# A state-space layer's rotation and scan, moved into the PSUM banks that hold their input

## The chip, the cores and the metric

The kernel runs on one core of a Trainium2 chip. The metric is device time in microseconds (us) of one execution of the whole program, which is a two-block network of which the state-space layer is the first stage. Five engines matter: TensorE (PE, matmuls, and PEld, its weight loads), VectorE (DVE), ScalarE (ACT), GpSimd (POOL) and SyncE (SP), which issues the DMAs.

## What is computed

The reference is two transformer-like blocks. Only the first mixer, the state-space layer, is touched:

```python
def s5_mixer(u, lam_re, lam_im, log_dt, b_re, b_im, c_re, c_im, d_skip, w_glu):
    lam = lax.complex(lam_re.astype(f32), lam_im.astype(f32))
    dt = jnp.exp(log_dt.astype(f32))[:, None]
    a_bar = jnp.exp(lam * dt)
    b_bar = ((a_bar - 1.0) / lam)[..., None] * lax.complex(b_re.astype(f32), b_im.astype(f32))
    ug = u.astype(f32).reshape(bsz, length, S5_GROUPS, S5_GROUP).astype(jnp.complex64)
    bu = jnp.einsum('blgh,gph->blgp', ug, b_bar)
    a_seq = jnp.broadcast_to(a_bar, bu.shape)
    _, states = lax.associative_scan(_ssm_combine, (a_seq, bu), axis=1)
    c = lax.complex(c_re.astype(f32), c_im.astype(f32))
    y = jnp.einsum('blgp,ghp->blgh', states, c).real.reshape(bsz, length, D_MODEL)
    y = y + d_skip.astype(f32) * u.astype(f32)
    y = jax.nn.gelu(y).astype(u.dtype)
    val, gate = jnp.split(y @ w_glu, 2, axis=-1)
    return val * jax.nn.sigmoid(gate)
```

Length 512, model width 1024, 64 groups of 16 channels with 64 complex states each, all in fp32. Behind this layer follow its gated projection (`w_glu`), a feed-forward layer, sparse attention, a second feed-forward layer and the second block.

## The kernel before

`s5` (line 1172 on) works in chunks of 8 tokens. The 512 tokens are 64 chunks, so the scan over time is a scan over 64 chunk states. The 64 groups are cut into four rounds q = 0 to 3 of 16 groups (two halves t of 8 groups on the two halves of the partitions). In each round:

- `input_tables(q)` (three DVE products at L1384 into `raw`, `wH`, `wL`, then two POOL sums, L1390 and L1391) makes the complex input matrix `B`.
- `chunk(q)` (PE) transposes `B` (`btps`, copied out by ACT at L1443) and multiplies it with the input `U`: the two banks `vps` hold the real and imaginary contribution of each chunk, as `s.V`.
- `rotation(q)` (five POOL operations, L1426 to L1430) makes `cos` and `sin`.
- `states(q)` (14 DVE operations, L1492 to L1505) rotates `s.V` by `cos` and `sin`, so that the scan has a real factor, scans the two parts (L1499), and rotates back; ACT then copies the results `vr`, `vi` into `W` (L1510).
- `output_tables(q)` makes three more products on DVE (L1384, into `wL`, `Qi`, `Qr`) and `sums` two on POOL.
- `outputs(q)` (PE, tiles `yps`) multiplies `W` with `Q` and `U` with `toep` in two banks of 512 columns, ACT applies the gelu (L1527).
- `by_feature(q)` transposes the result (`yt`), and ACT and DVE split it into `xH` and `xL` (L178, L179).
- `kernel_of(q)` (PE, tile `kps`, 16 small matmuls with 32 columns each) makes the short convolution, which ACT copies (L1481) and a DMA writes as `toep`.

The rounds are pipelined by the loop at the end of `s5`: pass q issues, in this order, `input_tables(q+1)`, the sums of Q(q), `rotation(q+1)`, `outputs(q-1)`, `chunk(q+1)`, `states(q)`, `output_tables(q+1)`, `by_feature(q-1)`, `kernel_of(q+1)`. `in_order` fixes that order on DVE, POOL, ACT and PE, so each engine takes its own part of it strictly in turn. On PE one pass is therefore `yps` of round q-1, `btps` and `vps` of q+1, `yt` of q-1, `kps` of q+1. The gated projection (tiles `lin`, L33 to L35) begins on PE behind `outputs(3)`.

PSUM has eight banks: tag `pj` has four (here `vps` and `yps`, later `lin`), `sc` two (here `kps` and, ahead of the loop, `xps`), `tp` two. Scratch tiles of `states` (`mid_tmp`) come from a pool of six.

Of the kernel before, what the change touches and what calls it, by code (L numbers as in the profile page):

```python
# [75 lines left out]
def ps(k, name, tag="tp"):  # L76
    return k.psum.tile([P, 512], F32, tag=tag, name=name, bufs={"pj": 4, "sc": 2, "tp": 2}[tag])


def tmp(k, name="t", dt=F32):  # L80
    return k.tmp.tile([P, 512], dt, tag="tmp", name=name)
# [1090 lines left out]
def s5(k, x, next_gain):  # L1172
    nc, a = k.nc, k.a
    G2 = 32
    with ExitStack() as es:
# [17 lines left out]
        for n in ("s5_b_re", "s5_b_im"):  # L1193
            t_ = ep.tile([G2, 2, 64, 16], F32, name=n)
            v = a[n][0].rearrange("(q t i) p h -> t q i (p h)", q=4, t=2)
# [90 lines left out]
        for f in range(2):  # L1286
            for m in (1, 2, 4):
                n = m if f == 0 else min(m, 7 - m)
# [81 lines left out]
        for g in range(8):  # L1370
            b = ps(k, "ups", "pj")
# [29 lines left out]
        def mid_tmp(name):  # L1401
            return tmp(k, name).rearrange("p (a b) -> p a b", a=8)

        def big(name, bufs):
            return qp.tile([P, 1024], F32, tag=name, name=name, bufs=bufs)
# [80 lines left out]
        def flat(t):  # L1486
            return t.rearrange("p a b -> p (a b)")

        def states(q):
            s = st_[q]  # L1490
            vr, vi, w1, w2 = [mid_tmp(n) for n in ("vr", "vi", "w1", "w2")]
            nc.vector.tensor_mul(vi, s.V[1], s.cos)  # L1492
            nc.vector.tensor_mul(w2, s.V[0], s.sin)
            nc.vector.tensor_mul(vr, s.V[0], s.cos)
            nc.vector.tensor_mul(w1, s.V[1], s.sin)
            nc.vector.tensor_sub(vi, vi, w2)
            nc.vector.tensor_add(vr, vr, w1)
            for v in (vi, vr):
                nc.vector.tensor_tensor_scan(flat(v), flat(s.dec), flat(v), 0.0, op0=ALU.mult, op1=ALU.add)  # L1499
            nc.vector.tensor_mul(w1, vi, s.sin)  # L1500
            nc.vector.tensor_mul(w2, vi, s.cos)
            nc.vector.tensor_mul(vi, vr, s.sin)
            nc.vector.tensor_mul(vr, vr, s.cos)
            nc.vector.tensor_add(vi, vi, w2)
            nc.vector.tensor_sub(vr, vr, w1)  # L1505

            for w, z, sign in zip(W[q % 2], (vr, vi), (1.0, -1.0)):
                for t in range(2):
                    rows = slice(t * 64, t * 64 + 64)
                    s.done = nc.scalar.activation(w[rows, :, t, 1:], z[rows, :, :63], AF.Copy, scale=sign)  # L1510

        def outputs(q):
            s = st_[q]

            s.y = big("y", 2).rearrange("p (j i h) -> p j i h", j=8, i=8)
            for hh in range(2):
                b = ps(k, "yps", "pj")
                for i4 in range(4):
                    i = hh * 4 + i4
                    o = b[:, i4 * P:(i4 + 1) * P]  # L1520
                    for ri in range(2):
                        nc.tensor.matmul(o, W[q % 2][ri][:, i].rearrange("p t c -> p (t c)"),
                                         s.Q[ri][:, i].rearrange("p t h -> p (t h)"), start=ri == 0, stop=False)
                    for t in range(2):
                        rhs = s.toep.rearrange("p j (t i h) -> p t i j h", t=2, h=16)[:, t, i]
                        nc.tensor.matmul(o[t * 64:(t + 1) * 64], U[2 * q + hh][:, i4, t], rhs, start=False, stop=True)
                nc.scalar.activation(s.y[:, :, hh * 4:hh * 4 + 4].rearrange("p j i h -> p i j h"),  # L1527
                                     b.rearrange("p (i j h) -> p i j h", i=4, j=8), AF.Gelu_apprx_tanh)
# [51 lines left out]
        for q in range(5):  # L1580
            if q < 3:
                input_tables(q + 1)
            if q < 4:
                st_[q].Q = sums(st_[q].Q, nc.gpsimd)
            if q < 3:
                rotation(q + 1, nc.gpsimd)
            if q:
                outputs(q - 1)
            if q < 3:
                constants_of(q + 1)  # L1590
                chunk(q + 1)
            if q < 4:
                states(q)
            if q < 3:
                decay(q + 1)
                output_tables(q + 1)
            if q:
                by_feature(q - 1)
            if q < 3:
                kernel_of(q + 1)  # L1600
# [3 lines left out]
    w = a["s5_w_glu"][0]  # L1604
# [118 lines left out]
```

## Time and profile before

| | us |
|---|---|
| median of three runs | 2055.54 |
| lowest and highest of them | 2047.66, 2055.92 |
| the profiled execution | 2055.45 |
| its span | 2053.7 |

The profile is of one execution. [...] The four rounds lie between 53 and 169 us of the span.

### The profile page before, as it was taken

The page shows a single profiled execution, that of the slowest core. Times are in us where ns is not written, and L with a number is a line of the kernel's source. Part 1 is how long each engine was busy: PE and PEld are TensorE (multiplying, and loading weights), DVE is VectorE, ACT ScalarE, POOL GpSimd, SP SyncE. Part 2 cuts the span into 40 slices and gives each one's busy share as a digit, 9 for nine tenths or more (in the row PEclk, how much of TensorE's full clock was granted, in tenths as well). Part 3 has the DMA queues.
Part 4 walks back from the last instruction along what each step waited for, and adds up shares of the span by engine and source line. Part 5 has one row for each costly group of instructions (what it writes and reads, how often), then busy time and mean ns, then how long its engine had stood idle before and what let it go on. Part 6 is the DMA issues. An engine that isn't in the chain of part 4 may idle for free. (4 is left out here: it accounts for less than half of the span.)

```text
span 2053.7 us, 25075 instructions
## 1 busy us (share of the span) xinstructions
PE 1905.5 (93%) x9383; PEld 1582.3 (77%) x9383; DVE 1166.4 (57%) x2082; ACT 818.7 (40%) x1461; POOL 454.6 (22%) x466
## 2 busy tenths in 40 slices
PE   4779999999998878999999999999999879999997
PEld 3657888888887867877888888877787658888886
DVE  8983444324357997787443334477776675333443
ACT  3333333213234437675322123355565364233232
POOL 6850111101114644533111011112221120000001
PEclk9668999999999989999999999999999889999999
DMA  3012333233323231222333232343232213332332
GB/s 77 24 45 93 94 93 101 93 102 93 97 83 83 57 89 43 57 61 77 102 93 102 93 103 87 98 131 92 77 93 72 80 34 93 97 98 93 103 93 82
DMA packets 183938, 173.44 MB, mean 84 GB/s; under 512 B 11953, under 2 KB 178297, under 8 KB 183816
## 3 DMA queue, kind: packets, MB, share of 16 engines
q1 hardware_dynamic: 183048, 170.98, 27.9%
q8 instruction: 74, 1.21, 0.2%
q0 software_dynamic: 768, 0.86, 0.2%
q14 instruction: 48, 0.39, 0.1%
HBM read 158.92 MB, written 2.13 MB: 78 GB/s over the span
## 5 line engine op out<-in xcount | busy, mean ns | idle before, releaser
L127 DVE TENSOR_TENSOR wL<-raw,wH 128x1024 fp32r<-128x1024 f32 (+4 forms) x282 | 327.8, 1163 | 470.3 <-ACT wH L126 470.0
L126 ACT ACTIVATE wH<-raw 128x1024 fp32r<-128x1024 f32 (+4 forms) x314 | 308.5, 984 | 586.7 <-PE lin L34 430.1
L33 PE MATMUL lin<-xH,wH 128*128 128x512 f32 x1312 | 518.1, 395 | 6.0 <-ACT wH L126 2.4
L35 PE MATMUL lin<-xH,wL 128*128 128x512 f32 x1312 | 514.3, 392 | 5.2 <-DVE wL L127 5.2
L34 PE MATMUL lin<-xL,wH 128*128 128x512 f32 x1312 | 514.6, 392 | 0.0
L33 PEld LDWEIGHTS lin<-xH,wH 128*128 128x128 f32 x1312 | 248.5, 189 | 57.7 <-ACT wH L126 4.6
L35 PEld LDWEIGHTS lin<-xH,wL 128*128 128x128 f32 x1312 | 247.6, 189 | 57.4 <-DVE wL L127 6.8
L34 PEld LDWEIGHTS lin<-xL,wH 128*128 128x128 f32 x1312 | 248.2, 189 | 49.9 <-issue 0.5
L35 PE MATMUL lin<-hH,wL 128*128 128x512 f32 x608 | 236.7, 389 | 0.0
L33 PE MATMUL lin<-hH,wH 128*128 128x512 f32 x608 | 236.6, 389 | 0.0
L34 PE MATMUL lin<-hL,wH 128*128 128x512 f32 x608 | 236.5, 389 | 0.0
L325 POOL TENSOR_TENSOR up<-up,ga 128x512 f32<-128x512 f32 x44 | 75.3, 1711 | 542.1 <-DVE up L324 542.1
L286 POOL TENSOR_TENSOR acc<-acc,sq 128x512 f32<-128x512 f32 x42 | 63.1, 1502 | 592.3 <-ACT sq L285 591.4
L34 PEld LDWEIGHTS lin<-hL,wH 128*128 128x128 f32 x608 | 114.1, 188 | 23.8
L33 PEld LDWEIGHTS lin<-hH,wH 128*128 128x128 f32 x608 | 114.1, 188 | 23.7
L35 PEld LDWEIGHTS lin<-hH,wL 128*128 128x128 f32 x608 | 114.1, 188 | 23.4
L33 PE MATMUL qkv<-wH,xH 128*128 128x384 f32 x256 | 91.7, 358 | 2.8 <-ACT sqv L662 2.8
L34 PE MATMUL qkv<-wL,xH 128*128 128x384 f32 x256 | 90.4, 353 | 1.3 <-POOL wL L127 1.3
L35 PE MATMUL qkv<-wH,xL 128*128 128x384 f32 x256 | 89.8, 351 | 0.0
L178 ACT ACTIVATE hH<-up 128x512 fp32r<-128x512 f32 x44 | 27.9, 633 | 147.5 <-POOL up L325 147.5
L179 DVE TENSOR_TENSOR hL<-up,hH 128x512 fp32r<-128x512 f32 x44 | 30.5, 692 | 88.0 <-ACT hH L178 88.0
L421 POOL TENSOR_SCALAR p<-p,r 128x128 f32<-128x128 f32 (+1 forms) x96 | 52.8, 567 | 121.8 <-DVE r L419 91.2
(456 smaller groups left out, 2941.9 us busy)
## 6 DMA issues: line engine op xcount, KB each, us to landing
raw<-in_ffn_w_gate_up SPq DMA_DIRECT2D x88, 512.0 KB
raw<-in_ffn_w_down SPq DMA_DIRECT2D x40, 512.0 KB
raw<-in_w_up SPq DMA_DIRECT2D x32, 512.0 KB
raw<-in_w_down SPq DMA_DIRECT2D x28, 512.0 KB
raw<-in_dsa_w_in SPq DMA_DIRECT2D x96, 128.0 KB
raw<-in_w_in SPq DMA_DIRECT2D x20, 512.0 KB
raw<-in_s_w_glu SPq DMA_DIRECT2D x16, 512.0 KB
k<-k SPq DMA_DIRECT2D x30, 256.0 KB
```

Of the source, the lines that this page charges most:

```text
L33: nc.tensor.matmul(out, wH, xH, start=start, stop=False)
L34: nc.tensor.matmul(out, wH, xL, start=False, stop=False)
L35: nc.tensor.matmul(out, wL, xH, start=False, stop=stop)
L126: nc.scalar.activation(wH, raw, AF.Copy)
L127: (l_engine or nc.vector).tensor_sub(wL, raw, wH.bitcast(F32))
L178: k.nc.scalar.activation(outH, src, AF.Copy)
L179: k.nc.vector.tensor_sub(outL, src, outH.bitcast(F32))
L286: (nc.vector if d == KT - 1 else nc.gpsimd).tensor_add(k.acc, k.acc, sq)
L325: nc.gpsimd.tensor_mul(u, u, acts[m])
L421: nc.gpsimd.tensor_scalar(p, p, r[:, b:b + 1], 1.0, op0=ALU.mult, op1=ALU.mult)
```

## The change

`states` no longer copies the rotated parts out to SBUF. It names the two PSUM banks of `s.V` A and B, writes two of the four products of the first rotation to scratch and the other two back into A and B, subtracts and adds into A and B, scans A and B in place, and rotates back with A and B as source and partly as target. There are 14 operations before and after. Each of them now has one input in PSUM and one in SBUF; eight write to PSUM. The scratch tile `w2` is gone. `outputs` takes its two banks from tag `sc` in place of `pj`.

```diff
         def states(q):
             s = st_[q]
-            vr, vi, w1, w2 = [mid_tmp(n) for n in ("vr", "vi", "w1", "w2")]
-            nc.vector.tensor_mul(vi, s.V[1], s.cos)
-            nc.vector.tensor_mul(w2, s.V[0], s.sin)
-            nc.vector.tensor_mul(vr, s.V[0], s.cos)
-            nc.vector.tensor_mul(w1, s.V[1], s.sin)
-            nc.vector.tensor_sub(vi, vi, w2)
-            nc.vector.tensor_add(vr, vr, w1)
-            for v in (vi, vr):
+            vr, vi, w = [mid_tmp(n) for n in ("vr", "vi", "w1")]
+
+            A, B = s.V
+            nc.vector.tensor_mul(vi, B, s.cos)
+            nc.vector.tensor_mul(vr, A, s.cos)
+            nc.vector.tensor_mul(A, A, s.sin)
+            nc.vector.tensor_mul(B, B, s.sin)
+            nc.vector.tensor_sub(A, vi, A)
+            nc.vector.tensor_add(B, vr, B)
+            for v in (A, B):
                 nc.vector.tensor_tensor_scan(flat(v), flat(s.dec), flat(v), 0.0, op0=ALU.mult, op1=ALU.add)
-            nc.vector.tensor_mul(w1, vi, s.sin)
-            nc.vector.tensor_mul(w2, vi, s.cos)
-            nc.vector.tensor_mul(vi, vr, s.sin)
-            nc.vector.tensor_mul(vr, vr, s.cos)
-            nc.vector.tensor_add(vi, vi, w2)
-            nc.vector.tensor_sub(vr, vr, w1)
+            nc.vector.tensor_mul(w, A, s.sin)
+            nc.vector.tensor_mul(A, A, s.cos)
+            nc.vector.tensor_mul(vi, B, s.sin)
+            nc.vector.tensor_mul(B, B, s.cos)
+            nc.vector.tensor_add(vi, vi, A)
+            nc.vector.tensor_sub(vr, B, w)
...
-                b = ps(k, "yps", "pj")
+                b = ps(k, "yps", "sc")
```

On DVE, round 0, the middle of `states` before (`vi`, `vr`, `w1`, `w2` are SBUF scratch, `vps` PSUM, `dec` the scan's factor in SBUF):

```order
L1495 TENSOR_TENSOR w1_761<-vps_551,sin_486 128x512
L1496 TENSOR_TENSOR vi_760<-vi_760,w2_762 128x512 [waits DVE_49]
L1497 TENSOR_TENSOR vr_759<-vr_759,w1_761 128x512 [waits DVE_49]
L1499 SCALAR_TENSOR_TENSOR vi_760<-dec_584,vi_760 128x512 [waits DVE_49,Activation_49]
L1499 SCALAR_TENSOR_TENSOR vr_759<-dec_584,vr_759 128x512 [waits DVE_49]
L1500 TENSOR_TENSOR w1_761<-vi_760,sin_486 128x512 [waits DVE_49]
```

and the same place now:

```order
L1497 TENSOR_TENSOR vps_551<-vps_551,sin_486 128x512
L1498 TENSOR_TENSOR vps_534<-vi_760,vps_534 128x512 [waits DVE_49]
L1499 TENSOR_TENSOR vps_551<-vr_759,vps_551 128x512 [waits DVE_49]
L1501 SCALAR_TENSOR_TENSOR vps_534<-dec_584,vps_534 128x512 [waits DVE_49,Activation_49]
L1501 SCALAR_TENSOR_TENSOR vps_551<-dec_584,vps_551 128x512 [waits DVE_49]
L1502 TENSOR_TENSOR w1_761<-vps_534,sin_486 128x512 [waits DVE_49]
```

The place in the program and the number of operations are the same; from the subtraction on, one of the two inputs of each is a PSUM bank where both were SBUF tiles. No instruction of POOL, ACT or SP moves.

On PE, the second half of `chunk(2)` before (`btps` are the transposes of `B`, `U4` and `U5` inputs):

```order
L1442 MATMUL btps_891<-ident_73,wH_820 128x128 [waits Activation_49]
L1442 MATMUL btps_891<-ident_73,wH_820 128x128 x3
L1442 MATMUL btps_897<-ident_73,wH_820 128x128 [waits Activation_49]
L1442 MATMUL btps_897<-ident_73,wH_820 128x128 x3
L1450 MATMUL vps_903<-U4_453,raw_877 64x64 x8
L1450 MATMUL vps_903<-U5_460,raw_877 64x64 x8
```

and now:

```order
L1442 MATMUL btps_890<-ident_73,wH_819 128x128 [waits Activation_49]
L1442 MATMUL btps_890<-ident_73,wH_819 128x128 x3
L1442 MATMUL btps_896<-ident_73,wH_819 128x128 [waits Activation_49]
L1442 MATMUL btps_896<-ident_73,wH_819 128x128 x3
L1450 MATMUL vps_902<-U4_453,raw_876 64x64 [waits DVE_49]
L1450 MATMUL vps_902<-U4_453,raw_876 64x64 x7
L1450 MATMUL vps_902<-U5_460,raw_876 64x64 x8
```

The order is the same; the first `vps` matmul of rounds 2 and 3 now waits until DVE has finished with the bank, which `states` of two rounds before holds to its end. The `yps` matmuls, in the other two banks, wait for ACT (the last reader of those) where they waited for DVE.

## Rows read from the trace of the kernel before

**Rows 1.** The page's first part: busy us, share, instructions.

```profile
PE 1905.5 (93%) x9383; PEld 1582.3 (77%) x9383; DVE 1166.4 (57%) x2082; ACT 818.7 (40%) x1461; POOL 454.6 (22%) x466
```

**Rows 2.** By windows: PE, PEld, DVE, ACT, POOL busy, PE clock, DMA.

```profile
76.80:91.80 15.00, 14.53 (x64) 9.81 (x64) 15.00 (x12) 4.14 (x7) 10.72 (x4) 0.50 0.13 39
...
105.20:116.10 10.90, 10.43 (x46) 7.15 (x46) 9.64 (x14) 4.24 (x10) 3.57 (x2) 0.50 0.19 55
116.10:118.40 2.30, 2.30 (x21) 1.59 (x20) 2.30 (x1) 0.00 (x0) 2.30 (x2) 1.00 0.03 4
...
173.50:250.00 76.50, 76.50 (x339) 63.31 (x338) 26.81 (x29) 25.41 (x31) 7.05 (x5) 1.00 0.32 103
```

**Rows 3.** Timeline of PE, 67 to 169 us: start, us, instruction, idle before.

```profile
67.72 0.39 PE L1479 MATMUL kps<-cbd,wH 128*128 128x32 f32 x2
76.78 0.77 PE L1522 MATMUL yps<-Qr,W 128*128 128x128 f32 x2 [8.67 <-issue]
...
91.82 1.97 PE L1442 MATMUL btps<-ident,wL 128*128 128x128 f32 x8
...
105.20 0.77 PE L1522 MATMUL yps<-Qr,W 128*128 128x128 f32 x2 [1.06 <-issue]
...
118.45 1.09 PE L1442 MATMUL btps<-ident,wL 128*128 128x128 f32 x8
...
136.56 0.77 PE L1522 MATMUL yps<-Qr,W 128*128 128x128 f32 x2 [7.07 <-issue]
...
154.13 0.63 PE L1522 MATMUL yps<-Qr,W 128*128 128x128 f32 x2
...
168.61 0.80 PE L33 MATMUL lin<-xH,wH 128*128 128x512 f32 x1
```

**Rows 4.** Waits, 45 to 170 us: us in total, times, longest.

```profile
ACT W L1510 <- DVE vr L1505: 32.6, 3, 13.0
```

**Rows 5.** Timeline of DVE, round 0 and the start of round 1.

```profile
53.55 0.68 DVE L1492 TENSOR_TENSOR vi<-vps,cos 128x512 f32<-128x512 f32 x1
...
55.94 2.78 DVE L1496 TENSOR_TENSOR vi<-vi,w 128x512 f32<-128x512 f32 x1
58.65 2.83 DVE L1497 TENSOR_TENSOR vr<-vr,w 128x512 f32<-128x512 f32 x1
61.41 3.38 DVE L1499 TENSOR_TENSOR_SCAN vi<-dec,vi 128x512 f32<-128x512 f32 x1
...
75.25 1.21 DVE L1384 TENSOR_TENSOR wL<-pw,cv 128x1024 f32<-128x1024 f32 x1
...
82.06 0.68 DVE L1492 TENSOR_TENSOR vi<-vps,cos 128x512 f32<-128x512 f32 x1
```

**Rows 6.** Timeline of POOL over the same stretch.

```profile
52.58 3.28 POOL L1390 TENSOR_TENSOR wH<-raw,wH 128x1024 f32<-128x1024 f32 x1 [3.60 <-DVE wH L1384]
55.82 2.36 POOL L1391 TENSOR_TENSOR wL<-raw,wL 128x1024 f32<-128x1024 f32 x1
58.13 2.81 POOL L1390 TENSOR_TENSOR Qi<-wL,Qi 128x1024 f32<-128x1024 f32 x1
...
63.67 2.37 POOL L1426 TENSOR_TENSOR r<-rt,rsum 128x512 f32<-128x512 f32 x1
...
71.87 1.70 POOL L1430 TENSOR_TENSOR sin<-r,sin 128x512 f32<-128x512 f32 x1
```

**Rows 7.** Timeline of DVE, round 3.

```profile
141.37 0.68 DVE L1492 TENSOR_TENSOR vi<-vps,cos 128x512 f32<-128x512 f32 x1
...
143.76 0.68 DVE L1496 TENSOR_TENSOR vi<-vi,w 128x512 f32<-128x512 f32 x1
...
144.96 1.21 DVE L1499 TENSOR_TENSOR_SCAN vi<-dec,vi 128x512 f32<-128x512 f32 x1
...
150.45 0.68 DVE L1505 TENSOR_TENSOR vr<-vr,w 128x512 f32<-128x512 f32 x1
```

**Rows 8.** Timeline of ACT, the first copies into W.

```profile
75.42 1.25 ACT L1510 ACTIVATE W<-vr 64x504 f32<-64x504 f32 x2 [13.01 <-DVE vr L1505]
```

**Rows 9.** Groups of DVE by line, 53 to 152 us: busy, mean ns | idle.

```profile
L179 DVE TENSOR_TENSOR xL<-yt,xH 128x256 fp32r<-128x256 f32 x8 | 3.2, 422 | 2.5 <-ACT xH L178 2.5
```

## The prediction

> **What bounds the kernel now.** Read the page first: PE is busy 93% of the span, DVE 57%, POOL 22% [rows 1]. So whatever shortens DVE work is worth nothing unless PE stands waiting for it. The view by windows then shows two regimes. From 173.5 us on PE is busy for the whole of each window at full clock (76.50 of 76.50 us); before that, in the four rounds of the state-space layer, it works at half clock for long stretches and has holes [rows 2]. Then read the timeline of PE for the holes. From the end of `kps` of round 1 at 67.72 + 0.39 = 68.11 us to the first `lin` matmul at 168.61 us there are three idle times worth the name: 8.67 us ahead of `outputs(0)`, 1.06 us ahead of `outputs(1)`, 7.07 us ahead of `outputs(2)`, 16.80 us in all [rows 3]. All three end when `W` is there: in this stretch ACT's copies into `W` waited three times for the last DVE operation of `states`, 32.6 us in total [rows 4]. The bound of the layer is thus the loop DVE `states` to ACT `W` to PE `outputs`, and what the change can take off the end is at first these 16.80 us. `lin` starts as soon as PE is through with `outputs(3)`, and behind it PE is full, so an earlier `lin` moves everything behind it.
>
> **Why states is slow.** The DVE timeline of round 0 has two kinds of rows. The four products that read a PSUM bank take 0.68 us, though POOL is working (its L1390 runs from 52.58 to 55.86 us). The subtraction and addition behind them, with both inputs in SBUF, take 2.78 and 2.83 us and the first scan 3.38 us [rows 5, 6]. Each stalled row ends about half a microsecond after a POOL instruction has ended: L1496 ends at 58.72, POOL's L1391 at 58.18 [rows 5, 6]. So the two engines take turns, one instruction each, at something that they share. In round 3, where POOL has nothing left to do, the very same rows take 0.68 and 1.21 us [rows 7]. The whole of `states` takes 150.45 + 0.68 - 141.37 = 9.8 us there, and 75.25 - 53.55 = 21.7 us in round 0, of which 12 us are stalls; rounds 1 and 2 look the same.
>
> **What the change removes.** After it every operation of `states` has one input in PSUM and one in SBUF. The row for that is the product from `vps`, which is not stalled [rows 5]. I take 9.8 us for each round, so `states` ends 12 us sooner in rounds 0 to 2. What the trace does not show is an operation that writes to PSUM, and a scan on it. The lower bound is the free row of the same shape, 0.68 us and 1.21 us for a scan; below that nothing goes, since the element count is unchanged. The upper bound is the stalled row, 2.8 and 3.4 us. I take the lower one, because reading PSUM at all costs nothing there: 0.68 us from PSUM against 0.68 us from SBUF [rows 5, 7].
>
> [...]
>
> **What comes late next: DVE and POOL.** The stalls don't vanish altogether, they move. `states(0)` now ends at 53.55 + 9.8 = 63.3 us. POOL's four sums run beside it without turns: 52.58 + 3.28 + 3 x 2.31 = 62.8 us (2.31 us is the unstalled row, 55.82 to 58.13) [rows 6]. Behind it DVE has six table products with both inputs in SBUF, 1.21 us each, and POOL the five rotation operations. These ran 63.67 to 73.57 us with turns taken; without the five DVE turns of 0.5 to 1 us in them I put them at 6.2 us. Taking turns, both need 6.2 + 6 x 1.21 = 13.5 us from 62.8, so `states(1)` starts near 76 us, where it was 82.06 [rows 5, 6]. At worst, rotation 9.9 us and then the tables 7.3 us, it is 80 us.
>
> **What comes late next: PE.** PE reaches `outputs(0)` at 68.1 us. It needs the first copies into `W`; ACT takes 1.25 us for the two [rows 8], so they are there at 63.3 + 1.3 = 64.6 us and PE no longer waits. The slack is 3.5 us. `outputs(0)` then takes its 15.04 us (76.78 to 91.82), to 83.2 us. `chunk(2)` behind it needs `B(2)`, two POOL sums (4.6 us) after 76, 80.6 us: no wait. `btps` to `kps` took 105.20 - 1.06 - 91.82 = 12.32 us, so PE is at 95.5 us when it comes to `outputs(1)`. `W(1)` is held back not by `states(1)` (76 + 9.8 = 85.8) but by ACT, which has the copies of `btps` ahead of it, to about 88 us; it is there by 89.3. So the second hole goes too. Next `outputs(1)`, 13.25 us (105.20 to 118.45), to 108.7 us. Meanwhile DVE has run round 1: tables and rotation as above, four `xL` pieces, (3.2 + 2.5) / 2 = 2.9 us [rows 9], and `input_tables(3)`, whose `wH` waits for `kps(2)` at 95.5; `states(2)` starts near 98 us. `W(2)` is ready by about 114 us, behind ACT's copies again; PE comes to `outputs(2)` at 108.7 + (136.56 - 7.07 - 118.45 = 11.04) = 119.7 us. The third hole goes. `outputs(2)`, `yt` and `outputs(3)` take 168.61 - 136.56 = 32.05 us, to 151.8 us [rows 3]. `states(3)`, which starts near 120 us behind `xL(1)`, ends near 130 us; ACT copies `W(3)` behind the gelu of `outputs(2)`, as before.
>
> The added waits are covered: `vps` of rounds 2 and 3 waits for the end of `states` two rounds before (63.3 against 83 us, 86 against 109), and `yps` in tag `sc` waits for `kps` or gelu copies that precede it on ACT by microseconds. If one of these failed, PE's whole queue would stand behind it; nothing in the times above comes closer than 3 us.
>
> **The sum.** 68.1 + 15.04 + 12.32 + 13.25 + 11.04 + 32.05 = 151.8 us for the first `lin`, in place of 168.6: 16.8 us less, exactly the three holes. Against the profiled execution, 2055.45 us, that is 2038.6 us; the median of the runs, 2055.54, is the same number. I say 2038.
>
> **The rivals.** (1) *PE's clock rises in `outputs`.* Its matmuls ran at 0.50 nearly throughout; only for the last 2.3 us of `outputs(1)`, 11 us after it had begun, was it 1.00 [rows 2]. `outputs(1)` was also the one that followed `kps` after only 1.06 us of idling, the two after 7 and 8.7 us stayed at half. With the holes gone all follow closely. At full clock one `outputs` takes about 8 us (two of its eight pieces took 2.0 us in those 2.3), 6.5 to 7 us less. One such stage gives 2031.5; if all four rise, DVE and POOL bound rounds 1 to 3 and `lin` starts near 138 us, 2025. The three times of before, one of them 8 us under the others, may be this. Against it: 32 us of closely packed `outputs(2)` and `outputs(3)` did not raise it.
>
> (2) *The turns take the place of the stalls.* If tables and rotation cost their upper bound each round, `states(1)` starts at 80, `states(2)` near 108, `states(3)` near 135 us and ends at 145; `W(3)` is there at 146, and `outputs(3)` begins at 146.5 in place of 154.1. Then 7.6 us are left of the gain: 2048. For it: all six tables have both inputs in SBUF. Against it: the turns in rows 5 and 6 cost DVE no more than the POOL instruction in front.
>
> (3) *It does not do what it says*: an operation with one SBUF input that writes to PSUM takes turns with POOL as before. Then nothing moves: 2055. The unstalled `vps` products speak against it.
>
> (4) *Slower.* The in-place banks have their own price: reading and writing one bank slows each PSUM-writing operation, in round 3 too, where nothing was stalled. Count six 512-column operations and two scans at two units each, ten units. The three uncontended rounds are then 3 x (9.8 + d) + 22 us of tables and `xL`, so `states(3)` ends at 53.55 + 51.4 + 3d + 9.8 + d = 115 + 4d. It ended at 151.1, so it decides from d = 9 us, 0.9 us a unit, on (0.6 now). At 1.2 us a unit, d = 12, `states(3)` ends at 163 us and the kernel takes about 2066. For it: no row shows such a write. Against: it must cost two and a half times a free operation.
>
> **How the numbers follow.** The forecast (2033 to 2044) gets 0.53, the rising clock (2024 to 2033) 0.23, the turns (2044 to 2051) 0.13, no effect (about 2055) 0.06, slower 0.05. About 0.5%, 10 us, is what a measurement of this kernel tells from no change. Faster by more than that (below 2045) is the forecast and the clock: 0.76; slower 0.05; the rest, 0.19, within. The range reaches down to 2026, leaving out the case that all four stages rise, and up to 2048, which takes in rival (2) and leaves (3) and (4) out.
>
> **What would show it.** The rows of `states` at 0.68 and 1.2 us in all four rounds (else rival 3 or 4); table products of up to 2.7 us beside POOL's rotation; the holes ahead of `outputs(0)`, `(1)` and `(2)` gone; the first `lin` at 152 us; the stretch behind it as long as before. The prediction is wrong if a hole stays, if the clock in `outputs` is not 0.50, or if the time from the first `lin` to the end changes by more than a few us.

## The result and the profile after

The changed kernel takes 2026.17 us (median of four runs, 2024.39 to 2026.96), beside 2053.97 us (2047.66 to 2055.92) for the kernel before: a ratio of 0.9874, 95% interval 0.9856 to 0.9891. That is 27.8 us less, where 16.8 us less were forecast: 2026.17 lies 0.17 us above the lower end of the range, in the band of rival (1) and not in the forecast of 2033 to 2044. The profiled execution took 2024.39 us with a span of 2022.6.

First the operations of `states`. The timeline of DVE, after, round 0, the scans of round 3 and the tables behind round 0 (start, us, instruction):

```profile
53.56 0.69 DVE L1494 TENSOR_TENSOR vi<-vps,cos 128x512 f32<-128x512 f32 x1
...
55.96 0.69 DVE L1498 TENSOR_TENSOR vps<-vi,vps 128x512 f32<-128x512 f32 x1
56.55 0.69 DVE L1499 TENSOR_TENSOR vps<-vr,vps 128x512 f32<-128x512 f32 x1
57.15 2.34 DVE L1501 TENSOR_TENSOR_SCAN vps<-dec,vps 128x512 f32<-128x512 f32 x2
...
62.97 2.36 DVE L1384 TENSOR_TENSOR wL<-pw,cv 128x1024 f32<-128x1024 f32 x1
65.25 2.48 DVE L1384 TENSOR_TENSOR Qi<-pw,cv 128x1024 f32<-128x1024 f32 x1
...
74.46 1.21 DVE L1384 TENSOR_TENSOR wL<-bw,bt 128x1024 f32<-128x1024 f32 x1
75.59 0.68 DVE L1494 TENSOR_TENSOR vi<-vps,cos 128x512 f32<-128x512 f32 x1
...
120.35 2.33 DVE L1501 TENSOR_TENSOR_SCAN vps<-dec,vps 128x512 f32<-128x512 f32 x2
```

The subtraction and addition take 0.69 us where they took 2.78 and 2.83, two scans together 2.34 us where the first alone took 3.38 [rows 5]. They are as fast in round 0, with POOL at work, as in round 3, where it is nearly done. `states(0)` takes 62.97 - 53.56 = 9.4 us in place of 21.7. The stalls have moved to the table products, 1.21 us before [rows 5], now 2.3 to 2.5 us five times out of six: those are the ones that lie beside POOL's rotation. `states(1)` starts at 75.59 us, before at 82.06.

POOL, after, the same stretch. Its sums, 2.81 us each when DVE took turns with them [rows 6], run at 2.35; rotation is what now takes turns:

```profile
58.16 2.35 POOL L1390 TENSOR_TENSOR Qi<-wL,Qi 128x1024 f32<-128x1024 f32 x1
...
62.78 1.46 POOL L1426 TENSOR_TENSOR r<-rt,rsum 128x512 f32<-128x512 f32 x1
64.21 2.44 POOL L1427 TENSOR_TENSOR sin<-rsum,rt 128x512 f32<-128x512 f32 x1
```

The timeline of PE, after, answers [rows 3]:

```profile
69.60 0.77 PE L1524 MATMUL yps<-Qr,W 128*128 128x128 f32 x2
...
80.26 1.09 PE L1442 MATMUL btps<-ident,wL 128*128 128x128 f32 x8 [0.22 <-POOL wL L1391]
...
90.85 0.47 PE L1524 MATMUL yps<-Qr,W 128*128 128x128 f32 x2
...
102.55 1.97 PE L1442 MATMUL btps<-ident,wL 128*128 128x128 f32 x8 [2.09 <-POOL wL L1391]
...
113.95 0.78 PE L1524 MATMUL yps<-Qr,W 128*128 128x128 f32 x2
...
127.64 0.46 PE L1524 MATMUL yps<-Qr,W 128*128 128x128 f32 x2 [1.45 <-issue]
...
141.14 0.50 PE L33 MATMUL lin<-xH,wH 128*128 128x512 f32 x1
```

No idle time stands ahead of `outputs(0)`, `(1)` and `(2)` any more; ahead of and inside `outputs(3)` PE still waits 1.45 and 0.77 us for `W(3)`. The first `lin` comes at 141.1 us, before at 168.6: 27.5 us, against 16.8 forecast. The other 3.6 us of the two profiles' spans (2053.7 and 2022.6) lie behind the first `lin`, 1885.1 us before and 1881.5 after. That is within the scatter of that stretch: a kernel of the old kind below (`x_sc`) has 2046.0 - 164.2 = 1881.8 us there, the changed kernel in a second profile 2023.9 - 139.2 = 1884.7, and all kept profiles lie between 1881.5 and 1885.1.

What the forecast did not have is in the view by windows, after, for the four `outputs` (PE, PEld, DVE, ACT, POOL busy, PE clock, DMA):

```profile
69.60:80.00 10.40, 10.40 (x65) 7.25 (x65) 10.40 (x11) 2.26 (x3) 9.24 (x4) 0.74 0.19 57
90.80:100.40 9.60, 9.60 (x66) 6.72 (x65) 8.70 (x13) 1.96 (x5) 7.02 (x5) 0.82 0.14 38
113.90:124.40 10.50, 10.50 (x66) 7.31 (x65) 9.60 (x17) 1.96 (x5) 7.53 (x4) 0.74 0.19 58
127.60:141.10 13.50, 12.69 (x64) 8.77 (x64) 3.78 (x6) 5.12 (x9) 0.00 (x0) 0.62 0.25 79
```

The stages took 15.0, 13.3, 15.1 and 14.5 us at a clock of 0.50 nearly throughout [rows 2, 3]. Now they take 10.4, 9.6, 10.4 and 13.5 us at mean clocks of 0.62 to 0.82, that is, part of each at a clock of 0.50 and part at 1.00, the full one in this view. `outputs(0)`, for one, had 0.50 from 69.6 to 73.2 us, and `outputs(1)` 1.00 from 90.8 to 92.0 and 0.50 from 92.0 to 94.0. The timelines show it by the pace of the first two matmuls of a piece, 0.80 us at 0.50 and 0.49 at 1.00; the very first two of a stage took 0.77 and 0.46 to 0.47.

### The profile page after: what moved, and what is told of

It reads as the page before. It is cut to its first block, busy times and chain, and to the rows that moved or that the text cites. A ratio compares the mean times of both kernels' runs of the same rounds, so it can differ in the third digit from the quotient of the medians.

```text
span 2022.6 us, 25073 instructions
## 1 busy us (share of the span) xinstructions
PE 1890.0 (93%) x9383; PEld 1571.9 (78%) x9383; DVE 1142.5 (56%) x2082; ACT 819.3 (41%) x1461; POOL 451.7 (22%) x466
## 3 DMA queue, kind: packets, MB, share of 16 engines
q8 instruction: 74, 1.21, 0.3%
```

## The experiments

My theory after the result had two parts. (a) A DVE operation with two SBUF inputs takes turns with POOL, instruction by instruction, and one with a PSUM input does not; the change takes `states` out of these turns, `W` comes earlier, and PE's holes close. (b) With the holes closed PE's clock rises within `outputs`, which gives the part that was not forecast. The rivals: the other banks for `yps` carry the gain; SBUF inputs are slow as such; the clock's rise has nothing to do with the holes.

### The banks: x_sc and x_pj

`x_sc` is the kernel before with the tag alone changed, `x_pj` the changed kernel with the tag alone taken back:

```diff
-                b = ps(k, "yps", "pj")
+                b = ps(k, "yps", "sc")
```

> The kernel before with one line changed: the yps banks come from tag sc. My theory (the gain comes from DVE operations that no longer take turns with POOL, and from what follows of it on PE) expects nothing here: states 21.7 us in rounds 0 to 2, the three PE holes of 8.7, 1.1 and 7.1 us, the first lin near 168.6 us, about 2054 us. The rival, that the other banks free the PE order, expects smaller holes and 5 us or more less.

> The changed kernel with the yps banks back in tag pj, so the four pj banks hold both vps and yps. vps of rounds 2 and 3 then has to wait for the end of states of the round just before (85.4 and 107.3 us in the changed kernel, where vps began at 83.6 and 106.0). Theory: 2 to 3 us more on PE, the states rows unchanged at 0.69 us, 2026 to 2030 us. Rival, that the move of yps carries the gain: 2045 us or more.

`x_sc` took 2053.3 us, ratio 0.9998 (0.9987 to 1.0010); `x_pj` 2027.73 us, 0.9873 (0.9854 to 0.9893). So the banks for `yps` carry nothing; the whole gain is in `states`. In `x_pj` the wait that I had expected for `vps` isn't there: `vps` of round 2 ran from 83.0 to 85.1 us without idling, and the first `lin` came at 140.6 us. Its `outputs` took 12.6, 13.7, 13.5 and 9.2 us, though PE had not idled ahead of any of them. `outputs(1)` even began at the pace of the full clock, 0.47 us, and then fell to 0.80; the same pair of matmuls in the first and in the second piece of the stage:

```profile
90.24 0.47 PE L1524 MATMUL yps<-Qr,W 128*128 128x128 f32 x2
...
91.41 0.80 PE L1524 MATMUL yps<-Qr,W 128*128 128x128 f32 x2
```

The profile of `x_sc` brought something else. Its `states` started at 53.55, 82.05, 113.42 and 141.35 us, as before, but its `outputs` took 12.0, 15.1, 11.2 and 11.8 us, the first `lin` came at 164.2 us, and that execution was the quickest of its ten, 2047.74 us. The holes ahead of the four stages were 9.73, 4.29, 5.30 and 2.90 us. Behind the longest of them `outputs(0)` began at the slow pace, 0.77 us, and went over to 0.49 half way:

```profile
76.77 0.77 PE L1522 MATMUL yps<-Qr,W 128*128 128x128 f32 x2 [9.73 <-issue]
...
84.69 0.49 PE L1522 MATMUL yps<-Qr,W 128*128 128x128 f32 x2
```

The length of `outputs` thus varies from execution to execution of one and the same kind of kernel, which fits the 8 us between the runs of the kernel before. It also varies with and without holes, so theory (b) can't be the whole of it.

### Which operations take turns: x_scan and x_rotb

In `x_scan` two of the 14 operations get two SBUF inputs again:

```diff
-            nc.vector.tensor_sub(A, vi, A)
-            nc.vector.tensor_add(B, vr, B)
-            for v in (A, B):
-                nc.vector.tensor_tensor_scan(flat(v), flat(s.dec), flat(v), ...
+            nc.vector.tensor_sub(vi, vi, A)
+            nc.vector.tensor_add(vr, vr, B)
+            for v, z in ((A, vi), (B, vr)):
+                nc.vector.tensor_tensor_scan(flat(v), flat(s.dec), flat(z), ...
```

> The changed kernel, but the subtraction and addition ahead of the scans write to SBUF scratch and the scans read both inputs there (output in the PSUM banks). Exactly two of the 14 operations of states then have two SBUF inputs. Theory (turns are taken per instruction, by its two SBUF inputs): these two rows 2.4 to 3.4 us in rounds 0 to 2 and 1.2 in round 3, the other twelve 0.69; states 13 us; PE has the slack, so the first lin moves by 0 to 3 us, 2025 to 2030 us. Rival (PSUM output, or all SBUF traffic, decides): the scans stay at 1.2 us, states 9.8 us.

The timeline of DVE in `x_scan`, round 0:

```profile
56.52 0.68 DVE L1499 TENSOR_TENSOR vr<-vr,vps 128x512 f32<-128x512 f32 x1
57.12 2.15 DVE L1501 TENSOR_TENSOR_SCAN vps<-dec,vi 128x512 f32<-128x512 f32 x1
59.18 3.31 DVE L1501 TENSOR_TENSOR_SCAN vps<-dec,vr 128x512 f32<-128x512 f32 x1
62.41 0.67 DVE L1502 TENSOR_TENSOR w<-vps,sin 128x512 f32<-128x512 f32 x1
```

Exactly the two scans are stalled, with their output in PSUM as in the changed kernel; their neighbours are not. Rounds 1 and 2 show the same (2.1 and 3.3 us). It is the inputs that decide. On the time I was wrong: 2035.4 us (2028.12 to 2038.3), ratio 0.9904 (0.9879 to 0.9929), not 2025 to 2030. In its profile, the quickest run, `states` started 1.9, 3.7 and 5.6 us later (77.5, 101.6, 122.4), the first `lin` came 2.8 us later, as expected, and `outputs(0)` and `(1)` took 14.8 and 13.8 us, though PE had not idled ahead of either. In `outputs(0)` it waited 0.45 us behind the first two matmuls, and the clock had fallen:

```profile
67.83 0.47 PE L1524 MATMUL yps<-Qr,W 128*128 128x128 f32 x2
68.75 0.80 PE L1524 MATMUL yps<-Qi,W 128*128 128x128 f32 x2 [0.45 <-ACT W L1512]
```

Why the median lost 8 us was not settled; longer `outputs` would fit.

`x_rotb` is the kernel before with the five operations of `rotation(q+1)` issued on DVE behind `output_tables(q+1)`; POOL keeps its four sums.

```diff
-            if q < 3:
-                rotation(q + 1, nc.gpsimd)
...
                 output_tables(q + 1)
+                rotation(q + 1, nc.vector)
```

> The kernel before with the same move of rotation to DVE, so that states, with all SBUF inputs, meets only POOL's sums and not rotation. Theory (one turn per POOL instruction): the stalls end when POOL's sums end, near 65 us in round 0; about 7 us of stalls are left of 12, states about 17 us; its starts at 80, 110 and 137 us, first lin 3 to 5 us earlier, 2048 to 2052 us. Rival (SBUF inputs are slow by themselves): states stays at 21.7 us and 3 us of rotation are added each round, 2060 us or more.

DVE, then POOL, in `x_rotb`, round 0:

```profile
61.42 3.39 DVE L1499 TENSOR_TENSOR_SCAN vi<-dec,vi 128x512 f32<-128x512 f32 x1
64.73 1.19 DVE L1499 TENSOR_TENSOR_SCAN vr<-dec,vr 128x512 f32<-128x512 f32 x1
65.85 0.66 DVE L1500 TENSOR_TENSOR w<-vi,sin 128x512 f32<-128x512 f32 x1
```

```profile
60.91 2.82 POOL L1391 TENSOR_TENSOR Qr<-wL,Qr 128x1024 f32<-128x1024 f32 x1
79.73 3.27 POOL L1390 TENSOR_TENSOR wH<-raw,wH 128x1024 f32<-128x1024 f32 x1 [16.00 <-DVE wH L1384]
```

POOL's last sum ends at 63.73 us, and with it the stalls: the scan that was waiting ends 1.1 us later, and the next takes 1.19 us where it had taken 2.41. All its inputs are still in SBUF. So SBUF inputs are not slow as such; POOL's working next to them is. `states(0)` took 69.68 - 53.56 = 16.1 us. The time did not move to 2048 to 2052 as I had said, 2053.53 us, ratio 0.9999 (0.9988 to 1.0010): rotation itself cost DVE 4.2 us from start to end, not 3.0, and 8.3 us in round 2, where its first two operations took 3.13 and 3.08 us, likely beside POOL's last two sums (see `x_rot`), so `states(3)` started less than 1 us earlier.

### Taking the remaining turns away: x_rot

The same move of rotation, in the changed kernel.

> The changed kernel, but the five operations of rotation(q+1) are issued on DVE behind output_tables(q+1) and no longer on POOL. POOL then has only its four sums, which lie beside states. Theory (the table products at 2.4 us are turns with rotation, six of them in round 0 and three in rounds 1 and 2): all products 1.2 us, 3.0 us more on DVE for rotation; states start at 72.8, 94.6 and 113 us in place of 75.6, 97.9 and 116.8; 2021 to 2025 us. Rival (products are slow for another reason): they stay at 2.4 us, states 3 us later each round, 2032 us or more.

All table products were 1.21 to 1.22 us, so the turns with rotation were indeed what slowed them. But rotation's first three operations took 1.03 to 1.05 us on DVE, not 0.68, in rounds 0 and 1, and in round 2 the moved rotation met turns of its own. There it followed directly on the products `Qi` and `Qr` that POOL's last two sums read (they ended at 108.48 and 109.62 us), and I take it that those sums ran beside it; their own times were not recorded. Its first two operations, which have two SBUF inputs, took three times as long:

```profile
109.54 3.12 DVE L1426 TENSOR_TENSOR r<-rt,rsum 128x512 f32<-128x512 f32 x1
112.59 3.09 DVE L1427 TENSOR_TENSOR sin<-rsum,rt 128x512 f32<-128x512 f32 x1
```

So `states` started at 73.9, 96.7 and 120.3 us (75.6, 97.9 and 116.8 in the changed kernel): earlier twice, and later where the turns came back. The kernel took 2031.84 us, ratio 0.9895 (0.9877 to 0.9912), not 2021 to 2025; the interval overlaps that of the changed kernel. Moving rotation buys little: of the 6 us that the turns cost in round 0, DVE has to spend 4 to be rid of them. Whether it would pay with rotation placed clear of the last sums was not tried.

### The clock: x_delay and x_fill

`x_delay` gives the changed kernel its late `W` back, without stalls:

```diff
-            nc.vector.tensor_sub(vr, B, w)
+            for _ in range(21 if q < 3 else 1):
+                nc.vector.tensor_sub(vr, B, w)
```

> The changed kernel, but the last operation of states is issued 21 times in place of once in rounds 0 to 2 (same result each time), which makes states about 21.7 us as before, without any stall. Theory (earlier W closes the PE holes, and the closed holes let PE's clock rise in outputs): the three holes return, outputs run at clock 0.50 again for 13 to 15 us, first lin 166 to 169 us, 2052 to 2056 us. Rival (the clock rises for another reason, such as the banks or the traffic): outputs stay near 10 us each, the holes are larger, first lin near 163 us, about 2048 us.

The view by windows for its four `outputs`:

```profile
79.00:93.30 14.30, 13.83 (x65) 9.36 (x65) 14.30 (x19) 4.14 (x7) 10.02 (x4) 0.54 0.14 42
109.70:124.00 14.30, 13.88 (x65) 9.41 (x66) 13.03 (x18) 4.17 (x10) 7.04 (x3) 0.54 0.17 48
143.30:158.30 15.00, 14.58 (x64) 9.81 (x64) 12.94 (x20) 4.16 (x10) 5.59 (x2) 0.50 0.15 43
160.80:175.30 14.50, 14.47 (x66) 9.75 (x65) 3.78 (x6) 4.51 (x8) 0.00 (x0) 0.50 0.23 73
```

The holes were back, 10.95, 3.85 and 6.82 us, and with them `outputs` of 14.3 to 15.0 us at 0.50 to 0.54, with the banks and the PSUM traffic of the changed kernel. This profile is of the slowest of ten executions, 2062.24 us; three took 2052.5 to 2053.2, and what their stages took was not recorded. The time was 2060.2 us, 1.0027 (1.0009 to 1.0045), above the 2052 to 2056 that I had said: a repeated subtraction takes 0.72 us, not 0.6, so `states` was 23.9 us long, and each round 2.2 us longer than before; the first `lin` came 6.7 us later than in the kernel before, at 175.3.

`x_fill` is the opposite: the kernel before, late `W` and all, with its holes filled.

```diff
+        def fill(n, tag="sc"):
+            b = ps(k, "fillps", tag)
+            for i in range(n):
+                nc.tensor.transpose(b[:, (i % 4) * P:(i % 4 + 1) * P], k.ident, k.ident)
...
             if q:
+                fill((0, 58, 42, 70, 38)[q])
                 outputs(q - 1)
```

> The kernel before, states stalled as ever, but PE's waits ahead of outputs(0) to (3) are filled with 58, 42, 70 and 38 transposes of the identity into a bank that nobody reads. So W comes as late as before; only PE's idling is taken away. Theory (closed holes let the clock rise): outputs of 8 to 11 us each, the starts of states unchanged (82, 113, 141 us), first lin near 163 us, bound by W(3) at 152 us; 2046 to 2050 us. Rival (the clock in outputs has nothing to do with the holes): 13 to 15 us each, first lin 168 us, 2052 to 2056 us.

It took 2048.09 us, ratio 0.9979 (0.9967 to 0.9991), and the first `lin` came at 164.3 us. By windows, its `outputs`:

```profile
77.10:86.00 8.90, 8.34 (x66) 5.74 (x64) 8.90 (x10) 3.89 (x7) 4.88 (x2) 1.00 0.23 67
105.30:120.10 14.80, 14.03 (x65) 9.50 (x65) 13.53 (x15) 4.23 (x10) 7.49 (x3) 0.56 0.19 55
142.50:150.50 8.00, 8.00 (x66) 5.67 (x64) 7.93 (x12) 0.60 (x1) 0.75 (x1) 1.00 0.27 78
156.30:164.40 8.10, 8.10 (x67) 5.76 (x65) 2.40 (x5) 1.49 (x3) 0.00 (x0) 1.00 0.41 129
```

Three stages ran at a clock of 1.00 throughout. The other one, `outputs(1)`, is as telling: there my 42 transposes were too few, and the timeline shows PE idle for 2.06 us ahead of it.

```profile
96.89 6.35 PE L1547 MATMUL fillps<-ident 128*128 128x128 f32 x42
105.29 0.46 PE L1522 MATMUL yps<-Qr,W 128*128 128x128 f32 x2 [2.06 <-issue]
107.58 0.80 PE L1522 MATMUL yps<-Qr,W 128*128 128x128 f32 x2
```

Its first matmuls still ran at full clock (0.46 us a pair), then the clock fell (0.80 us), and stayed down to the end of the stage. So what PE does just ahead of `outputs` does matter, and the rival that the clock has nothing to do with it is out. But the hole is not all of it. Over all kept profiles, those of the next section too, the stages sort like this:

| just ahead of the stage | stages | took, us | mean |
|---|---|---|---|
| PE idle, 1.01 to 10.95 us | 19 | 11.2 to 15.1 | 13.5 |
| `kps`, no idle time | 18 | 8.1 to 14.9 | 11.7 |
| transposes that nobody reads, at most 0.32 us idle between | 8 | 8.0 to 9.2 | 8.4 |

The other eleven follow `yt` or `vps` without idle time: nine took 8.1 to 9.2 us, and two 14.5, where the clock was low already in the stage before. Behind idle time no stage was short; without it some were and some were not. Four kernels with the holes (before, `x_sc`, `x_rotb`, `x_delay`) took 50 to 58 us for their four stages, five without holes and without such transposes (changed, `x_after`, `x_pj`, `x_scan`, `x_rot`) 42 to 50. What decides within a row of the table, and when the clock rises within a stage, stays open.

The clock alone was worth only 5 us to the kernel before, since `W` bound it there.

### Making use of it: x_after, x_warm3, x_order, x_order_warm, x_warm

`x_after` is the changed kernel again; `x_warm3` adds 14 transposes ahead of `outputs(3)` alone; `x_warm` adds 16, 16, 16 and 14 ahead of all four. `x_order` issues `kernel_of(q+1)` ahead of `chunk(q+1)`, so that `kps` no longer stands directly ahead of `outputs`; `x_order_warm` adds 28 transposes ahead of `outputs(3)` to that.

> The changed kernel itself once more, beside the three that follow. In its profile outputs took 10.4, 9.6, 10.4 and 13.6 us: each began at clock 0.50 behind kps (the last behind a wait) and rose after 4 to 5 us, the last not until its end. If that is steady, the same within 2 us, 2024 to 2028 us; if the rise is partly chance, other lengths between 8 and 15 us and a spread of 5 us or more.

> The changed kernel, with 14 such transposes in the wait between yt(2) and outputs(3), where PE idled 1.45 and 0.77 us and outputs(3) then took 13.5 us. Theory: outputs(3) takes 8 to 10.5 us, first lin at 136 to 139 us, 2021 to 2024 us. Rival (the clock of a stage is chance): 13 to 14 us as before, or no shift of the median, 2025 to 2028 us.

> The changed kernel with kernel_of(q+1) issued ahead of chunk(q+1), so that on PE the small kps matmuls, in which the clock fell, no longer stand directly ahead of outputs; btps, vps and yt do. Theory (the clock in outputs is the one that the work just ahead leaves): outputs(1) and (2) start at 1.00 and take 8 to 9 us, outputs(0) and (3), behind a wait, 8 to 13; states starts as in the changed kernel (75.6, 97.9, 117); 2021 to 2026 us. Rival (chance): lengths as in the changed kernel, 2024 to 2030 us.

> The same, and 28 transposes of the identity fill PE's wait for W(3) ahead of outputs(3). Theory: outputs(3) takes 8 us as well, the first lin comes 8.5 us after W(3), near 136 us, and the runs spread less; 2018 to 2022 us. Rival: no shift against the changed kernel.

> The changed kernel in its own order, with 16, 16, 16 and 14 such transposes directly ahead of outputs(0) to (3), 2 to 4 us of extra PE work each in the first three. Theory: outputs 8 to 9 us each, so the extra work is paid back and the first lin comes at 136 to 139 us with little spread, 2019 to 2024 us. Rival (the clock does not follow the work ahead): outputs 10 to 14 us and the extra work on top, 2030 us or more.

| | `outputs(0)` to `(3)`, us | first `lin` | median us (range) | ratio (interval) |
|---|---|---|---|---|
| `x_after` | 8.1, 11.1, 13.5, 9.2 | 139.2 | 2027.31 (2023.97 to 2032.68) | 0.9882 (0.9863 to 0.9901) |
| `x_warm3` | 13.3, 8.1, 13.8, 8.1 | 140.2 | 2026.05 (2020.14 to 2029.16) | 0.9864 (0.9845 to 0.9884) |
| `x_order` | 8.8, 8.3, 8.1, 14.8 | 149.1 | 2033.52 (2032.15 to 2036.63) | 0.9911 (0.9895 to 0.9928) |
| `x_order_warm` | 9.1, 8.1, 8.2, 13.6 | 150.3 | 2032.77 (2030.49 to 2038.12) | 0.9907 (0.9889 to 0.9925) |
| `x_warm` | 8.3, 8.1, 8.1, 9.2 | 136.8 | 2020.97 (2020.07 to 2026.08) | 0.9854 (0.9833 to 0.9875) |

In the changed kernel the rise differs from execution to execution: two profiles give 10.4, 9.6, 10.4, 13.5 and 8.1, 11.1, 13.5, 9.2 us for the same four stages. (I had read all four of the first as beginning at 0.50; `outputs(1)` and `(3)` began at full clock, 0.47 and 0.46 us a pair, and fell.) In `x_warm3` the stage behind the filler took 8.1 us as expected, but two others took over 13 us in that execution, and the median did not move. In `x_order` and `x_order_warm` the stages that follow `vps` or `yt` took 8.1 to 9.1 us, and those behind a wait (4.32 and 1.66 us ahead of `outputs(3)`) 14.8 and 13.6. They lost all the same against the changed kernel: with `kps` ahead, the copies of `btps`, and on ACT behind them `W`, come later (in `x_order` `btps` of round 1 began at 65.69 us in place of 58.90, and PE waited until 72.70 us for the second pair of copies into `W(0)`, which in the changed kernel ended at 65.92), DVE waited 3.4 us there for the copies of `yt(0)`, and `states(2)` started at 101.4 and 104.0 us in place of 97.9.

`x_warm` has all four stages near 8 us:

```profile
70.50:78.70 8.20, 8.20 (x64) 5.80 (x64) 8.20 (x9) 0.60 (x1) 7.04 (x4) 0.99 0.20 60
94.90:103.00 8.10, 8.08 (x65) 5.76 (x65) 8.10 (x11) 0.60 (x1) 5.95 (x3) 1.00 0.26 75
116.00:124.10 8.10, 8.08 (x64) 5.67 (x64) 7.65 (x13) 1.30 (x3) 5.50 (x3) 1.00 0.25 75
127.70:136.80 9.10, 8.32 (x64) 5.81 (x64) 3.78 (x6) 5.09 (x9) 0.00 (x0) 1.00 0.34 107
```

The work that nobody reads, 2.0 to 3.6 us in each of the first three rounds, pays itself back, and its last part lies in a wait. The median is the lowest of all kernels here, 6 us under that of `x_after`; the two intervals against the kernel before overlap, but four of its five runs are faster than any of the ten of the changed kernel.

## Why the prediction came out as it did

**The bound and the cause: right.** PE waited for `W`, `W` for `states`, and `states` for turns with POOL. `x_rotb` and `x_scan` show the turns, and which operations take part in them. One reading was loose: the stalled scan ends 1.1 us behind POOL's instruction, not half a microsecond, about its own unstalled 1.2 us.

**The price of in-place PSUM operations: right.** I took the lower bound, 0.68 and 1.21 us; measured 0.69, and 2.34 us for two scans. `states` took 9.4 us, 9.8 were forecast. Next to a working POOL the operations of a round cost 12 us more with their operands in SBUF: 21.7 us in round 0 before, 9.4 now.

**What DVE and POOL do next: right in two rounds of three.** `states` started at 75.6, 97.9 and 116.8 us; 76, 98 and 120 were forecast. In the last I let DVE wait for `yt(1)` behind an `outputs(1)` of 13 us, which took 9.6. One wait that I had not counted came: `chunk(3)` waited 2.09 us for `B(3)`, because PE was ahead of time. The upper bound of this step, rival (2), did not come about; the turns took back 6 us of the 12 in round 0, and those lay beside PE's work.

**The three holes: right.** All 16.8 us of them are gone, and none of the added waits for banks showed.

**The length of `outputs`: wrong, and this is nearly the whole miss.** The sum took the four stages over at 15.04, 13.25, 15.1 and 14.45 us, 57.8 in all; they took 10.4, 9.6, 10.4 and 13.5, 43.9. That is 13.9 us; the wait for `B(3)` and the smaller gaps give 3 back, and 10.7 us are left between the forecast first `lin` (151.8) and the measured one (141.1). The rest of the distance to the profiled 2024.39 us is the scatter behind `lin`. I had the rise as rival (1), with 0.23, and had seen in the rows that `outputs(1)`, after the smallest hole, was the one that rose. But I weighed the long low-clock stretch of `outputs(2)` and `(3)` more heavily, without asking what stood ahead of it: a hole of 7 us. `x_fill` shows that filling such a hole with work ends the low clock (`outputs(2)` took 8.0 us at 1.00 there), and no stage behind idle time took under 11.2 us. That closing the holes is what raised the clock here is likely, not shown stage by stage: `x_pj` and `x_scan`, without holes, still had stages of 12 to 15 us.

**The number: inside the range by luck.** I named 2038, and my own sign of being wrong came true: the clock in `outputs` was not 0.50 but 0.62 to 0.82. That 2026.17 lies in the range is owed to a lower end set at 2026, just under it, for a rival that I thought less likely than the forecast.

**Whether all of this was the change's doing.** `x_pj` and `x_sc` say that `states` alone did it, and `x_delay`, with the new `states` but its old length or a little more, lost the whole gain.

## What to carry to other kernels

Where VectorE and GpSimd work side by side, look at whether a VectorE operation has two SBUF inputs: here, with one of them left in PSUM, the subtraction and addition no longer waited for GpSimd (0.69 us in place of 2.78 and 2.83), and the stall moved to the two-input SBUF work that was left (table products of 2.3 to 2.5 us in place of 1.21). When a change closes idle time ahead of a stretch of TensorE work, price the stretch at both clock levels (here about 8 us a stage at 1.00 and 15 at 0.50), look at which one its own start had, and take more than one profile, since the same kernel showed both (`outputs(3)` of the changed kernel 13.5 us at a mean clock of 0.62 and 9.2 at 1.00); idle time may then cost twice (behind it no stage here took under 11.2 us). Where TensorE must wait anyway, or small matmuls stand ahead of a long stage, a few useless transposes are worth a try: in `x_warm` they cost less than the low clock behind them (2020.97 us beside 2027.31).

## What the runs showed of the hardware

- Next to a working GpSimd, VectorE operations of `states` with two SBUF inputs took 1.6 to 2.8 us for 512 columns, against 0.66 to 0.69 without it, and GpSimd's sums beside them took 2.81 us, against 2.35: the two took turns. Those with one SBUF and one PSUM input took 0.69 us next to a working GpSimd, also when they wrote to the bank that they read. Scans likewise: two from PSUM took 2.34 us together next to a working GpSimd, one from SBUF 2.1 to 3.4 us, against 1.2 without it.
- TensorE ran `outputs` in 8.0 to 9.2 us directly behind transposes that nobody reads (8 stages of 8), at a clock of 0.99 or 1.00 in the seven for which the view was taken (`x_fill`, `x_warm`). Behind idle times of 1.01 to 10.95 us the same stage took 11.2 to 15.1 us (19 of 19), in some executions at 0.50 from start to end (15.0 us in `x_delay`). Behind `kps`, without idle time, it went either way, 8.1 to 14.9 us, from execution to execution.
- On VectorE the rotation's first three products, with broadcast and strided inputs, took 1.03 to 1.05 us for 512 columns while GpSimd was idle, its plain sums 0.68 to 0.69 (`x_rot`, `x_rotb`).
